# Weight sums of a seven-product step moved from VectorE into adding transfers, with two column sums and one weight split reordered

## The chip, the cores and the metric

The kernel runs on one core of a Trainium2 chip. The metric is the device time of one execution in microseconds (us). A difference of 0.2% is 2.2 us.

## The reference

One layer of an encoder on 256 tokens of width 2048, in float32: a mixer with two groups of eight heads (forgetting attention, "FoX", and stick-breaking attention, "SB"), and a convolutional feed-forward part.

```python
def reference(x, attn_norm, w_in, ..., w_out, ffn_norm, w_up, conv_w, conv_b, w_down):
    for layer in range(DEPTH):                                   # DEPTH = 1
        h = rms_norm(x, attn_norm[layer])
        x = x + hybrid_mixer(h, w_in[layer], ..., w_out[layer])
        h = rms_norm(x, ffn_norm[layer])
        x = x + conv_ffn(h, w_up[layer], conv_w[layer], conv_b[layer], w_down[layer])
    return x

def hybrid_mixer(...):
    ...
    merged = jnp.concatenate([rms_norm(from_heads(out_a), out_norm_fox_l),
                              rms_norm(from_heads(out_b), out_norm_sb_l)], axis=-1)
    return merged @ w_out_l          # (256 x 2048) @ (2048 x 2048)

def conv_ffn(h, w_up_l, conv_w_l, conv_b_l, w_down_l):
    u = h @ w_up_l
    ...                              # causal convolution of width 3
    gate, val = jnp.split(u, 2, axis=-1)
    return (jax.nn.silu(gate) * val) @ w_down_l
```

The change lies in `merged @ w_out_l`, in the rows of w_out that belong to the second group of heads (SB), and in the start of `conv_ffn` right behind it.

## The kernel before, in words

**Matmuls in three passes.** Each operand is split into a high part in a reduced format (`w_hi`, `hT[..., 0, :]`) and a low part, the rest (`w_lo`). A product is high x high, low x high and high x low. For weights the high part is a cast on ScalarE (ACT, L263) and the low part a subtraction on VectorE (DVE, L271), of 128 x 2048 elements each. `in_three` (L291) issues the matmuls on TensorE (PE, and PEld for its weight loads).

**Steps.** The program is a list of steps, one for each piece of weights of 1 MB. A step has a load (on SyncE's queue, SP), perhaps a sum, a split, its matmuls and a "follow", which adds the result to the residual stream `xb` (called `x2` in the code). The loop at the end of the kernel emits for step n: follows that are due, the split of step n + 2 (`SPLIT`), follows again, the load of step n + 6 (`LOAD`), the sum of step n + 4 (`SUM`), then the matmuls of step n, then the transposes that are due (`after`) and a part of the heads (`tick`). Each engine works through its own list in that order.

**w_out in two groups.** Group 0 is FoX, group 1 is SB. Each group's 1024 rows of w_out are multiplied with 2048 columns, in two halves of columns. Columns 0 and 1 (of 512 each, called c=0 and c=1 here) are done plainly in group 1, with the tile `acc_o`, in two steps each (`out_rows`, kh = 0 and 1). Columns 2 and 3 are done by `out_unit` in Strassen's manner: seven products instead of eight, on sums of weight blocks (w11, w12, w21, w22, 1 MB each) and sums of head outputs (`T5`, `S2`, `S4`, `T7`, kept in `oFox` and split into `hT`). In group 1 the steps come in this order, and I call the seven products P1 to P7:

| step of group 1 | work | weights before |
|---|---|---|
| 0 | P1 (bank "a") | w11 |
| 1, 2, 3 | c=0 first half, c=1 first half, c=0 second half (in which the heads end) | plain |
| 4 | P2 (bank "b"), T5 | w11 += w12, by an adding transfer |
| 5 | P3 (bank "bc") | w21 |
| 6 | P4 (bank "a"), S2 | w11 += w22, on DVE (L924) |
| 7 | c=1 second half | plain |
| 8 | P5 (bank "a"), T7 | w12 += w22, by an adding transfer |
| 9 | P6 (bank "b"), S4 | w22 |
| 10 | P7 (bank "a") | w11 += w21, by an adding transfer |

An adding transfer is a DMA on POOL's software queue (`q0` in the profile; L890 for weights, L956 for `xb`) that adds what it brings to what lies there. SP's loads are on a hardware queue (`q1`).

**The norm of the heads.** After c=0's second half, `norm_of_heads` takes the sum of squares on PE (`pg`, L968), works out the factor `rg` on DVE and ACT (`rs_a` L168 to `rg` L176) and its negative `nrg` (L974). Every addition to `xb` needs it. For P1, c=0, P2 and P3 the addition is staged: ACT writes the scaled bank into a `stage` tile (L955) and an adding transfer brings it to `xb`. For c=1 and for P4 to P7, DVE does it (L1035 and L913).

**Into the feed-forward.** When a column of `xb` is finished, `columns_done` has PE transpose it (L192; I write T c0 to T c3; they come in the order c0, c1, c3, c2), ACT squares it (L210), and ACT and DVE make the parts of `hT` (L200, L203). The transposes stand on PE in this place: c=1 second half, T c0, P5, P6, T c1, P7, T c3, then the first piece of w_up (FFN+0, L1252), T c2, and the next pieces.

Of the kernel before, what the change touches and what calls it, by code (L numbers as in the profile page):

```python
# [15 lines left out]
P = 128  # L16
# [29 lines left out]
def hybrid_layer(  # L46
# [219 lines left out]
    def split(raw, a, b):  # L266
        return subtracted(raw, *cast(raw, a * b, act.copy), a, b)
# [36 lines left out]

    def pieces(w, k0, n, c0, cols, matmuls, follow=None, hold=None):

        mem = {}

        def loads():
            mem["raw"] = load(rows_of(w, k0, n, c0, cols))  # L310

        def prepare():
            if hold is None:
                mem["parts"] = split(mem["raw"], n, cols)
            else:
# [554 lines left out]
    def out_unit(group, c0, raw_tokens):  # L870
# [9 lines left out]

        def product(name, new, lhs, weights, to, load_=(), sums=None, plus=None, negative=False, first=False, then=None,
                    finished=None, later=None, staged=False):
            parts = []
            n, t = to

            def loads():
                for key, src in load_:
                    mem[key] = load(src)
                if plus is not None:
                    nc.gpsimd.dma_start(  # L890
                        mem[weights].rearrange("p (a b) -> p a b", a=4), plus, accum_op=ALU.add
                    )

            def prepare():
                parts.extend(split(mem[weights], 4, 512))

# [21 lines left out]

            if later is not None:
                later.append(prepare)  # L920
            new_step(loads, sums, prepare if later is None else None, matmuls, follow)

        def sum_of(other):
            return lambda: dve.tensor_tensor(mem["11"], mem["11"], mem[other], op=ALU.add) and None  # L924

        later = later_splits
        if group == 0:
# [4 lines left out]
            yield product("b", False, fox_sum(S4), "22", (1, 0))  # L932
            yield product("a", False, fox_sum(T7), "12", (1, 1), plus=w22, negative=True)
            yield product("a", False, raw_tokens(1, 1), "11", (0, 1), plus=w21)
# [12 lines left out]
    later_splits, stages = [], []  # L947

    def add_by_transfer(xs, bank, r):
        if not stages:  # L950
            for t in (at.tile([P, WF], F32, name=f"stage{i}", tag=f"v{i}") for i in range(2)):
                stages.extend((t[:, :512], t[:, 512:]))
            stages.append(heads_tile("stage").rearrange("p a b -> p (a b)")[:, :512])
        stage = stages.pop()
        act.activation(stage, bank, AF.Identity, scale=r)  # L955
        nc.gpsimd.dma_start(xs, stage, accum_op=ALU.add)  # L956
# [42 lines left out]
    def out_rows(group, c, kh):  # L999
# [24 lines left out]
        def follow():  # L1024
# [51 lines left out]

    def sums_of_first_heads():
# [4 lines left out]
        yield  # L1082
# [436 lines left out]
```

## Time and profile before

| | us |
|---|---|
| three runs | 1101.57, 1102.04, 1102.05 (median 1102.04) |
| profiled execution | 1101.38 |
| its span on the core | 1099.6 |
| PE busy | 1088.7 (99%) |
| DVE busy | 938.1 (85%) |
| ACT busy | 766.1 (70%) |
| POOL busy | 67.4 (6%) |

Times in the profile are in us from the span's start. An idle time in brackets at a row's end is what the engine waited just before it, with what released it. The stage of the change is from about 330 to 405 us; the feed-forward follows and runs to the end.

### The profile page before, as it was taken

The page shows a single profiled execution, that of the slowest core. Times are in us where ns is not written, and L with a number is a line of the kernel's source. Part 1 is how long each engine was busy: PE and PEld are TensorE (multiplying, and loading weights), DVE is VectorE, ACT ScalarE, POOL GpSimd, SP SyncE. Part 2 cuts the span into 40 slices and gives each one's busy share as a digit, 9 for nine tenths or more (in the row PEclk, how much of TensorE's full clock was granted, in tenths as well). Part 3 has the DMA queues.
Part 4 walks back from the last instruction along what each step waited for, and adds up shares of the span by engine and source line. Part 5 has one row for each costly group of instructions (what it writes and reads, how often), then busy time and mean ns, then how long its engine had stood idle before and what let it go on. Part 6 is the DMA issues. An engine that isn't in the chain of part 4 may idle for free.

```text
span 1099.6 us, 14723 instructions
## 1 busy us (share of the span) xinstructions
PE 1088.7 (99%) x5689; PEld 937.4 (85%) x5689; DVE 938.1 (85%) x933; ACT 766.1 (70%) x984; POOL 67.4 (6%) x61
## 2 busy tenths in 40 slices
PE   9999999999999989999999999999999999999998
PEld 9988888888888778888888888888888888888887
DVE  5988899888899876779888998889898898879996
ACT  6767696767766866767766766776676667666762
POOL 0000000001000200000000010000000000000000
PEclk9999999999999999999999999999999999999999
DMA  8897886868778895569979598996979699895995
GB/s 308 282 273 227 267 217 189 245 192 271 237 218 222 199 286 187 166 192 224 309 203 310 173 276 258 249 287 175 299 203 274 235 240 296 199 317 167 287 262 146
DMA packets 177519, 262.98 MB, mean 239 GB/s; under 512 B 4760, under 2 KB 98346, under 8 KB 177450
## 3 DMA queue, kind: packets, MB, share of 16 engines
q1 hardware_dynamic: 151690, 210.26, 56.3%
q0 software_dynamic: 25584, 51.65, 26.7%
q8 instruction: 45, 0.74, 0.3%
q14 instruction: 24, 0.20, 0.0%
q10 hardware_dynamic: 176, 0.14, 0.0%
HBM read 258.62 MB, written 2.10 MB: 237 GB/s over the span
## 4 chain that ended last, share of the span: by engine, by line
PE 95%; DVE 2%; ACT 1%; issue 1%; DVEq 0%
PE pu L1252 44%; PE bank_a L291 19%; PE bank_b L291 11%; PE bank_c L291 6%; PE acc_v L411 4%; PE acc_o L291 3%; PE bank_e L291 2%; PE acc L291 2%; DVE w_lo L271 1%; ACT w_hi L263 1%; PE ps_h L637 1%; PE ps_o L709 1%; DVE hT L203 0%; PE ps_x L192 0%; PE ps_z L785 0%
## 5 line engine op out<-in xcount | busy, mean ns | idle before, releaser
L271 DVE TENSOR_TENSOR w_lo<-w_raw,w_hi 128x2048 fp32r<-128x2048 f32 (+2 forms) x254 | 562.5, 2219 | 119.4 <-ACT w_hi L263 115.9
L263 ACT CAST w_hi<-w_raw 128x2048 fp32r<-128x2048 f32 (+2 forms) x254 | 470.1, 1854 | 219.6 <-PE pu L1252 94.4
L1252 PE MATMUL pu<-hT,w_hi 128*128 128x512 f32 x1408 | 335.8, 391 | 2.1 <-DVE hT L203 2.0
L1252 PEld LDWEIGHTS pu<-hT,w_hi 128*128 128x128 f32 x1408 | 263.3, 188 | 57.1 <-DVE hT L203 3.0
L1252 PEld LDWEIGHTS pu<-hT,w_lo 128*128 128x128 f32 x1408 | 180.5, 192 | 6.7
L1252 PE MATMUL pu<-hT,w_lo 128*128 128x256 f32 x1408 | 182.4, 283 | 0.0
L1305 POOL DMA_DIRECT2D w_raw<-in_w_down_dram x31 | 39.9, 1305 | 664.8 <-DVE w_lo L271 318.7
L1176 ACT ACTIVATE tap<-up,ccol 128x256 f32<-128x256 f32 x176 | 74.7, 495 | 0.0
L291 PE MATMUL bank_a<-w_hi,hT 128*128 128x512 f32 x208 | 52.7, 395 | 1.3 <-ACT w_hi L263 1.3
L291 PEld LDWEIGHTS bank_a<-w_hi,hT 128*128 128x128 f32 x208 | 38.0, 188 | 9.0 <-ACT w_hi L263 1.7
L291 PE MATMUL bank_b<-w_hi,s 128*128 128x512 f32 x160 | 40.0, 392 | 0.0
L291 PE MATMUL bank_a<-w_hi,s 128*128 128x512 f32 x160 | 40.0, 392 | 0.0
L291 PE MATMUL bank_a<-w_hi,g 128*128 128x512 f32 x152 | 38.0, 392 | 0.0
L411 PE MATMUL acc_v<-w_hi,hT 128*128 128x344 f32 x192 | 35.5, 326 | 0.0
L291 PEld LDWEIGHTS bank_b<-w_hi,s 128*128 128x128 f32 x160 | 28.9, 189 | 5.2
L291 PEld LDWEIGHTS bank_a<-w_hi,s 128*128 128x128 f32 x160 | 28.9, 189 | 5.3
L1181 DVE TENSOR_TENSOR gate<-gate,tap 128x512 f32<-128x512 f32 x44 | 30.3, 688 | 2.3
L1181 DVE TENSOR_TENSOR val<-val,tap 128x512 f32<-128x512 f32 x44 | 30.3, 688 | 2.3
L1162 DVE TENSOR_TENSOR up<-t,R 128x512 f32<-128x512 f32 x44 | 30.5, 692 | 1.5
L291 PEld LDWEIGHTS bank_a<-w_hi,g 128*128 128x128 f32 x152 | 27.4, 189 | 5.0
L1169 ACT ACTIVATE gate<-up,ccol 128x256 f32<-128x256 f32 x44 | 24.1, 594 | 10.1 <-DVE s L1223 5.2
L411 PEld LDWEIGHTS acc_v<-w_hi,hT 128*128 128x128 f32 x192 | 30.3, 188 | 0.6 <-DVE hT L203 0.2
(314 smaller groups left out, 1432.9 us busy)
## 6 DMA issues: line engine op xcount, KB each, us to landing
w_raw<-in_w_up_dram SPq DMA_DIRECT2D x88, 1024.0 KB, 8.2
w_raw<-in_w_down_dram SPq DMA_DIRECT2D x44, 1024.0 KB, 7.0
w_raw<-in_w_in_dram SPq DMA_DIRECT2D x40, 1024.0 KB, 5.6
w_raw<-in_w_down_dram POOLq DMA_DIRECT2D x31, 1024.0 KB, 9.7
w_raw<-in_w_out_dram SPq DMA_DIRECT2D x16, 1024.0 KB, 7.6
w_raw<-in_w_in_dram POOLq DMA_DIRECT2D x10, 1024.0 KB, 9.5
w_raw<-in_w_in_dram SPq DMA_DIRECT2D x13, 516.0 KB, 5.2
w_raw<-in_w_out_dram POOLq DMA_DIRECT2D x5, 1024.0 KB, 9.2
```

Of the source, the lines that this page charges most:

```text
L263: copy(hi[:, :n], raw[:, :n])
L271: dve.tensor_tensor(lo[:, :n], raw[:, :n], f32(hi[:, :n]), op=ALU.subtract)
L291: nc.tensor.matmul(o, lhs(i, l, t), r[:, i, :] if cut is None else r[:, i, cut], start=starts and j == 0, stop=stops and j == 3 * n - 1, s ...
L411: nc.tensor.matmul(banks[j][t][:, :VC], of_half(hT[:, k], l, t), w[:, 0, m * VC : (m + 1) * VC], start=k == l == 0 and w is mem["parts", i ...
L637: nc.tensor.transpose(ps[:, h, :], rows[n, t][:, h * HD : (h + 1) * HD], ident)
L709: mm(po, v, w[:, i, :S], start=m == 0, stop=False)
L1162: dve.tensor_tensor(u[:, :, 2:], t2, R, op=ALU.mult)
L1169: act.activation(a[:, j, :], u[:, j, 2:], AF.Identity, scale=ccol[:, 2, f : f + 1], bias=ccol[:, 3, f : f + 1],)
L1176: act.activation(taps[w][:, j, :], u[:, j, w : w + S], AF.Copy, scale=ccol[:, w, f : f + 1])
L1181: dve.tensor_tensor(a, a, tap, op=ALU.add)
L1252: nc.tensor.matmul(acc[:, j, S:] if low else acc[:, j, :], (lo if low else hi)[:, i, j * P : (j + 1) * P], hT[:, k, 0, :] if low else hT[: ...
L1305: nc.gpsimd.dma_start(mem[weights].rearrange("p (a b) -> p a b", a=4), plus, accum_op=ALU.add)
```

## The change

**Weight sums.** P2's weights get a tile of their own ("5"): w11 is loaded a second time and w12 is added to it by a transfer. P4's weights become w11 + w12 + w22, by two adding transfers on the tile "11" (so the head sums and the bank signs stay as they are), and the sum on DVE goes. POOL's additions of weights in group 1 go from three to five, SP's loads of w_out from 16 to 17. P7's w21 comes later on the same tile, as before.

On POOL, at the place of the second heads, these rows stood before (`w_raw_2851` is the tile "11", `w_raw_3134` the tile "12", the last 2851 the addition of w21; `xb<-stage` is a staged sum):

```order
L890 DMA w_raw_2403<-in_w_out_dram 128x4x512
L890 DMA w_raw_2851<-in_w_out_dram 128x4x512
L890 DMA w_raw_3134<-in_w_out_dram 128x4x512
L956 DMA xb_2502<-stage_3244 128x512
L956 DMA xb_2502<-stage1_3243 128x512 x2
L890 DMA w_raw_2851<-in_w_out_dram 128x4x512
L956 DMA xb_2502<-stage0_3242 128x512 x2
```

And these stand there now (`w_raw_2968` is the new tile "5"):

```order
L892 DMA w_raw_2403<-in_w_out_dram 128x4x512
L892 DMA w_raw_2851<-in_w_out_dram 128x4x512
L892 DMA w_raw_2968<-in_w_out_dram 128x4x512
L892 DMA w_raw_2851<-in_w_out_dram 128x4x512
L892 DMA w_raw_3136<-in_w_out_dram 128x4x512
L965 DMA xb_2502<-stage0_3244 128x512 x2
L965 DMA xb_2502<-stage1_3245 128x512
L892 DMA w_raw_2851<-in_w_out_dram 128x4x512
L965 DMA xb_2502<-stage1_3245 128x512
L965 DMA xb_2502<-stage2_3246 128x512 x2
L965 DMA xb_2502<-stage0_3244 128x512
```

**Additions of c=1.** They are staged too, like those of c=0 (`if group:` instead of `if group > c:`), in six `stage` tiles that go round. On ACT, from the squares of c=0 to the squares of c=3, the order moves like this (the plain `w_hi<-w_raw` rows are casts of weights):

```order
 L210 ACTIVATE spare,ss_122<-xb 128x512 x2
+L964 ACTIVATE stage_3246<-acc_o,rg_126 128x512
+L964 ACTIVATE stage_3244<-acc_o,rg_126 128x512
 L200 ACTIVATE hT<-ps_x,pcol 128x256 x4
-L263 CAST w_hi<-w_raw 128x2048 x2
+L263 CAST w_hi<-w_raw 128x2048
 L210 ACTIVATE spare,ss_122<-xb 128x512 x2
+L263 CAST w_hi<-w_raw 128x2048
 L200 ACTIVATE hT<-ps_x,pcol 128x256 x2
 L263 CAST w_hi<-w_raw 128x2048
```

The two stagings of c=1 now stand ahead of c=0's `hT`; the cast of FFN+0's weights, which stood ahead of the squares of c=1, stands behind them. These squares and T c1 on PE now wait for the two adding transfers of c=1.

**Norm ahead of low weights, and other turns.** P3's cast comes early, and its low part is taken only behind the norm (`late_low`). The head sums of P4 run as its sum (`first_heads_sums`). Follows of group 1's products and of c=1 are put first in their turn (`first`). P7's split is taken at P5's follow and FFN+0's at P6's, out of one list (`later_splits`). On DVE, from the last head sums to P4's low weights, before:

```order
L1087 TENSOR_TENSOR oFox_114<-oFox_114 128x4x128
L1089 SCALAR_TENSOR_TENSOR oFox_114<-oFox_114 128x4x128
L1073 TENSOR_TENSOR hT_94<-oFox_114,hT_94 128x4x128
L271 TENSOR_TENSOR w_lo_3228<-w_raw_3020,w_hi_3227 128x2048
L168 TENSOR_SCALAR rs_a_3231<-pg_3220 128x2
L173 TENSOR_TENSOR rs_u_3233<-rs_a_3231,rs_y_3232 128x2
L174 TENSOR_TENSOR rs_u_3233<-rs_u_3233,rs_y_3232 128x2
L175 TENSOR_SCALAR rs_u_3233<-rs_u_3233 128x2
L176 TENSOR_TENSOR rg1_126<-rs_y_3232,rs_u_3233 128x2
L974 TENSOR_SCALAR nrg1_128<-rg1_126 128x2
```

And the same place now (`w_raw_3022` is P3's tile, `pg` the norm's sums):

```order
L1095 TENSOR_TENSOR oFox_114<-oFox_114 128x4x128
L1082 TENSOR_TENSOR hT_94<-oFox_114,hT_94 128x4x128
L1098 SCALAR_TENSOR_TENSOR oFox_114<-oFox_114 128x4x128
L168 TENSOR_SCALAR rs_a_3233<-pg_3226 128x2
L173 TENSOR_TENSOR rs_u_3235<-rs_a_3233,rs_y_3234 128x2
L174 TENSOR_TENSOR rs_u_3235<-rs_u_3235,rs_y_3234 128x2
L175 TENSOR_SCALAR rs_u_3235<-rs_u_3235 128x2
L176 TENSOR_TENSOR rg1_126<-rs_y_3234,rs_u_3235 128x2
L983 TENSOR_SCALAR nrg1_128<-rg1_126 128x2
L271 TENSOR_TENSOR w_lo_3186<-w_raw_3022,w_hi_3185 128x2048
```

P3's low weights (`w_lo` from tile 3020, now 3022) went from the place ahead of the norm to the place behind it. PE's instructions and their order are the same in both kernels; only what they wait for differs.

The diff, cut to what changes behaviour:

```diff
-    def pieces(w, k0, n, c0, cols, matmuls, follow=None, hold=None):
+    def pieces(w, k0, n, c0, cols, matmuls, follow=None, hold=None, first=False):
...
-        new_step(loads, None, prepare, lambda: matmuls(mem["parts"]), follow)
+        new_step(loads, None, prepare, lambda: matmuls(mem["parts"]), follow, first)
...
             def loads():
                 for key, src in load_:
                     mem[key] = load(src)
-                if plus is not None:
+                for src in plus:
                     nc.gpsimd.dma_start(
-                        mem[weights].rearrange("p (a b) -> p a b", a=4), plus, accum_op=ALU.add
+                        mem[weights].rearrange("p (a b) -> p a b", a=4), src, accum_op=ALU.add
                     )
             def prepare():
-                parts.extend(split(mem[weights], 4, 512))
+                if late_low:
+                    hi, lo = cast(mem[weights], 2048, act.copy)
+                    later.append(lambda: parts.extend(subtracted(mem[weights], hi, lo, 4, 512)))
+                else:
+                    parts.extend(split(mem[weights], 4, 512))
...
-            if later is not None:
+            if late:
                 later.append(prepare)
-            new_step(loads, sums, prepare if later is None else None, matmuls, follow)
+            new_step(loads, sums, None if late else prepare, matmuls, follow, first=group == 1)
...
+        def next_later():
+            later.pop(0)()
...
         yield product("a", True, raw_tokens(0, 0), "11", (0, 0), [("11", w11)], staged=True)
-        yield product("b", True, fox_sum(T5), "11", (1, 1), plus=w12, staged=True)
-        yield product("bc", True, raw_tokens(1, 0), "21", (0, 0), [("21", w21)], staged=True, later=later)
-        yield product("a", False, fox_sum(S2), "11", (1, 0), [("22", w22)], sum_of("22"), negative=True)
+        yield product("b", True, fox_sum(T5), "5", (1, 1), [("5", w11)], plus=[w12], staged=True)
+        yield product("bc", True, raw_tokens(1, 0), "21", (0, 0), [("21", w21)], staged=True, late_low=True)
+        yield product("a", False, fox_sum(S2), "11", (1, 0), sums=first_heads_sums, plus=[w12, w22], negative=True)
         yield product(
-            "a", False, fox_sum(T7), "12", (1, 1), [("12", w12)], plus=w22, negative=True,
-            then=lambda: later.pop()(),
+            "a", False, fox_sum(T7), "12", (1, 1), [("12", w12)], plus=[w22], negative=True, then=next_later,
         )
-        yield product("b", False, fox_sum(S4), "22", (1, 0), finished=3)
-        yield product("a", False, raw_tokens(1, 1), "11", (0, 1), plus=w21, finished=2, later=later)
+        yield product("b", False, fox_sum(S4), "22", (1, 0), [("22", w22)], then=next_later, finished=3)
+        yield product("a", False, raw_tokens(1, 1), "11", (0, 1), plus=[w21], finished=2, late=True)
...
         if not stages:
-            for t in (at.tile([P, WF], F32, name=f"stage{i}", tag=f"v{i}") for i in range(2)):
-                stages.extend((t[:, :512], t[:, 512:]))
-            stages.append(heads_tile("stage").rearrange("p a b -> p (a b)")[:, :512])
-        stage = stages.pop()
+            tiles = [at.tile([P, WF], F32, name=f"stage{i}", tag=f"v{i}") for i in range(2)]
+            tiles.append(heads_tile("stage2").rearrange("p a b -> p (a b)"))
+            stages.extend(t[:, c : c + 512] for t in tiles for c in (0, 512))
+        stage = stages.pop(0)
+        stages.append(stage)
...
-                if group > c:
+                if group:
                     add_by_transfer(xs, acc[t], rgs[group][:, t : t + 1])
...
-            held if (group, c, kh) == (0, 3, 0) else None,
+            held if (group, c, kh) == (0, 3, 0) else None, first=group == c == 1,
...
         high_sum(first_heads, last_tokens)
+        low_sum(first_heads, last_tokens)
         dve.scalar_tensor_tensor(a22, a11, -1.0, a22, op0=ALU.mult, op1=ALU.subtract)
-        low_sum(first_heads, last_tokens)
-        later_splits.pop(0)()
         yield
+        later_splits.pop()()
...
-    hooks[SB_OUT + 2] = lambda: following.append(sums_of_first_heads())
+    later_splits.append(steps[FFN][2])
+    steps[FFN] = steps[FFN][:2] + (None,) + steps[FFN][3:]
```

More of the change, by code (lines that the diff above doesn't have):

```diff
@@ L879, in open_bank, with product @@
             return psb.tile([P, 512], F32, name=f"bank_{name}", tag="t")
-        def product(name, new, lhs, weights, to, load_=(), sums=None, plus=None, negative=False, first=False, then=None,
-                    finished=None, later=None, staged=False):
+        def product(
+            name, new, lhs, weights, to, load_=(), sums=None, plus=(), negative=False, first=False, then=None,
+            finished=None, late_low=False, late=False, staged=False,
+        ):
             parts = []
@@ L932, in out_unit @@
             yield product("b", False, fox_sum(S4), "22", (1, 0))
-            yield product("a", False, fox_sum(T7), "12", (1, 1), plus=w22, negative=True)
-            yield product("a", False, raw_tokens(1, 1), "11", (0, 1), plus=w21)
+            yield product("a", False, fox_sum(T7), "12", (1, 1), plus=[w22], negative=True)
+            yield product("a", False, raw_tokens(1, 1), "11", (0, 1), plus=[w21])
             return
         yield product("a", True, raw_tokens(0, 0), "11", (0, 0), [("11", w11)], staged=True)
-        yield product("b", True, fox_sum(T5), "11", (1, 1), plus=w12, staged=True)
-        yield product("bc", True, raw_tokens(1, 0), "21", (0, 0), [("21", w21)], staged=True, later=later)
-        yield product("a", False, fox_sum(S2), "11", (1, 0), [("22", w22)], sum_of("22"), negative=True)
+        yield product("b", True, fox_sum(T5), "5", (1, 1), [("5", w11)], plus=[w12], staged=True)
+        yield product("bc", True, raw_tokens(1, 0), "21", (0, 0), [("21", w21)], staged=True, late_low=True)
+        yield product("a", False, fox_sum(S2), "11", (1, 0), sums=first_heads_sums, plus=[w12, w22], negative=True)
         yield product(
-            "a", False, fox_sum(T7), "12", (1, 1), [("12", w12)], plus=w22, negative=True,
-            then=lambda: later.pop()(),
-        )
-        yield product("b", False, fox_sum(S4), "22", (1, 0), finished=3)
-        yield product("a", False, raw_tokens(1, 1), "11", (0, 1), plus=w21, finished=2, later=later)
+            "a", False, fox_sum(T7), "12", (1, 1), [("12", w12)], plus=[w22], negative=True, then=next_later,
+        )
+        yield product("b", False, fox_sum(S4), "22", (1, 0), [("22", w22)], then=next_later, finished=3)
+        yield product("a", False, raw_tokens(1, 1), "11", (0, 1), plus=[w21], finished=2, late=True)
     later_splits, stages = [], []
@@ L1075, in low_sum, with first_heads_sums @@
         )
-    def sums_of_first_heads():
+    def first_heads_sums():
         a11, a21 = oFox[:, first_heads, first_tokens], oFox[:, first_heads, last_tokens]
@@ L1081, in sums_of_first_heads @@
         dve.tensor_tensor(a11, a11, a21, op=ALU.subtract)
-        yield
     def sums_of_heads():
```

## The prediction

> **What bounds the kernel now.** I read the page's busy times first, then the chain that ended last, then the stretches of the stage that the change touches, and only then single rows and transfers.
>
> ```profile
> PE 1088.7 (99%) x5689; PEld 937.4 (85%) x5689; DVE 938.1 (85%) x933; ACT 766.1 (70%) x984; POOL 67.4 (6%) x61
> ...
> PE 95%; DVE 2%; ACT 1%; issue 1%; DVEq 0%
> ```
>
> TensorE (PE) works 99% of the span and carries 95% of the chain, and the change leaves PE's own instructions and their order alone. So time can be won only where PE idles, and lost only where a new wait stops it. In the next table, of stretches in the w_out products of the second heads, the columns are the stretch, its length, then busy time of PE, PEld, DVE, ACT and POOL, the granted clock, the DMA share and GB/s.
>
> ```profile
> 352.00:361.70 9.70, 9.70 (x47) 8.09 (x46) 6.43 (x12) 3.95 (x7) 0.03 (x1) 1.00 0.68 113
> 361.70:369.35 7.65, 5.12 (x20) 3.25 (x19) 4.37 (x6) 7.62 (x10) 3.57 (x5) 1.00 0.78 196
> 369.35:381.00 11.65, 11.65 (x55) 9.77 (x56) 11.65 (x13) 9.75 (x13) 2.19 (x3) 1.00 1.05 195
> 381.00:388.00 7.00, 5.28 (x32) 4.29 (x31) 7.00 (x6) 6.75 (x13) 0.00 (x0) 1.00 1.09 357
> 388.00:400.00 12.00, 10.07 (x58) 8.08 (x56) 10.87 (x23) 8.57 (x18) 0.00 (x0) 1.00 1.08 336
> 400.00:405.00 5.00, 4.85 (x23) 4.11 (x24) 0.63 (x3) 1.86 (x2) 0.00 (x0) 0.66 1.02 328
> 405.00:500.00 95.00, 95.00 (x548) 84.03 (x547) 68.08 (x65) 63.67 (x85) 2.62 (x2) 1.00 0.59 180
> ```
>
> PE is never idle up to 361.7 and from 405 on. It idles 7.65 - 5.12 = 2.53 us in the second row, 1.72 in the fourth and 1.93 in the fifth; the sixth runs at a clock of 0.66. These 6.2 us and that clock are all there is to win. The first piece, and what ends it (rows of the timeline: start, length, engine, line; in brackets the idle time and its releaser):
>
> ```profile
> 357.41 0.50 PE L968 MATMUL pg<-cs,ssq 128*128 128x1 f32 x4
> 358.08 2.29 DVE L271 TENSOR_TENSOR w_lo<-w_raw,w_hi 128x2048 fp32r<-128x2048 f32 x1 [1.12 <-ACT w_hi L263]
> 360.29 0.15 DVE L168 TENSOR_SCALAR rs_a<-pg 128x2 f32<-128x2 f32 x1
> 361.73 0.69 ACT L955 ACTIVATE stage<-bank_a,rg 128x512 f32<-128x512 f32 x1 [0.82 <-DVE rg L176]
> 364.79 2.11 PE L291 MATMUL bank_a<-w_hi,hT 128*128 128x512 f32 x8 [1.27 <-ACT w_hi L263]
> 367.11 1.20 PE L291 MATMUL bank_a<-w_lo,hT 128*128 128x512 f32 x4 [0.22 <-DVE w_lo L271]
> 369.35 3.92 PE L291 MATMUL acc_o<-w_hi,oSb 128*128 128x512 f32 x16 [1.04 <-ACT w_hi L263]
> ```
>
> The norm's sums of squares are finished on PE at 357.41 + 0.50 = 357.9, but DVE is in P3's low weights until 360.37, so `rs_a` starts at 360.29 and the staging of P1 at 361.73. P4 then starts 1.27 us late, its low pass 0.22 late and the c=1 rows 1.04 late.
>
> **The change part by part.**
>
> Norm ahead of P3's low weights: that 2.29 us instruction leaves the place ahead of `rs_a`, which can start at 358.0 instead of 360.29, and the norm and the staging behind it come 2.3 us earlier. Low bound of the gain: 0, if the cast of P4 waits for something else (its sum now comes from two adding transfers). High bound: all 2.53. P3's low weights move behind the norm: done at about 359.4 + 2.3 = 361.7, and P3's low pass reads them at 362.44, so that costs nothing, with 0.7 us of cover; gone, it would be the low pass that is late. The c=1 cast still stands behind three stagings on ACT, so I take P4's 1.27 and the 0.22, together 1.5, and keep the 1.04 for the bound.
>
> ```profile
> 343.30 1.91 ACT L263 CAST w_hi<-w_raw 128x2048 fp32r<-128x2048 f32 x1
> 347.56 2.29 DVE L924 TENSOR_TENSOR w_raw<-w_raw 128x2048 f32<-128x2048 f32 x1
> 348.14 0.47 ACT L828 ACTIVATE oSb<-ps_o,pcol 128x256 fp32r<-128x256 f32 x1 [2.94 <-PE ps_o L710]
> ```
>
> The weight sum on DVE (2.29 us at 347.56) goes. PE lost nothing to it, since PE is fully busy there, so it is worth 0. The price of its replacement: P2's cast, at 343.30 before, now reads a tile that is loaded (w11 again) and then added to. ACT waits 2.94 us ahead of `oSb` of a head at 348.14, so the cast of 1.91 may start as late as 346.2 at no cost; later than that, the last head's outputs, and with them the norm, are late by as much. When does that addition land? Software transfers of before:
>
> ```profile
> q0 software_dynamic: 528, 1.05, 86.4%
> w_raw<-in_w_out_dram POOLq DMA_DIRECT2D x1, 1024.0 KB, 8.4
> q1 hardware_dynamic: 1489, 2.96, 99.5%
> q0 software_dynamic: 528, 1.05, 53.0%
> q0 software_dynamic: 466, 0.86, 43.8%
> q1 hardware_dynamic: 1040, 1.05, 27.3%
> q0 software_dynamic: 773, 1.49, 93.3%
> q1 hardware_dynamic: 395, 0.40, 15.6%
> ```
>
> These are the software (q0) and hardware (q1) queues in 333 to 340, in 340 to 348, in 348 to 360, in 360 to 372 and in 372 to 381, with the packets, the MB and the share of the 16 DMA engines; the second row is the addition issued at 331.86, which lands 8.4 us later, at 340.3. In 372 to 381 the two shares add to 1.09, so 1.1 is what a full stretch reads. One addition of 1.05 MB takes 0.530 x 12 / 1.1 to 0.864 x 7 / 1.1 = 5.5 to 5.8 of engine time, and 1.49 MB in 0.933 x 9 / 1.1 = 7.6 is 5.1 per MB; I use 5.2 us per MB. The new addition follows that of 340.3: alone it lands at 340.3 + 5.5 = 345.8; taking turns with the loads, which fill 340 to 348 (99.5%), at up to 347.9. The middle, 346.8, holds the cast 0.6 us. Bounds 0 and 1.7. So the work ahead of T c1 (PE's transposes of the c=1 columns) comes 1.5 - 0.6 = 0.9 us earlier, between -1.7 and 2.53.
>
> P4's two additions land 5.5 and 11 us later, at 351 to 353 and 357 to 359. P4's cast ended just ahead of 364.79 and so began at 362.9, 2.3 earlier now: 360.6. So nothing waits for these two, nor for P5's behind them, but they fill the queue for all that follows.
>
> The additions of c=1 are what I think decides. Before, DVE did them; now ACT stages the two halves and two adding transfers bring them to `xb`:
>
> ```profile
> 378.00 1.40 DVE L1035 SCALAR_TENSOR_TENSOR xb<-acc_o,rg,xb 128x512 f32<-128x512 f32 x2
> 365.67 1.26 ACT L955 ACTIVATE stage<-acc_o,rg 128x512 f32<-128x512 f32 x2
> 375.56 1.57 ACT L200 ACTIVATE hT<-ps_x,pcol 128x256 fp32r<-128x256 f32 x4 [0.70 <-PE ps_x L192]
> 381.26 1.03 PE L192 MATMUL ps_x<-cs,xb 128*128 128x128 f32 x8
> 381.93 0.62 ACT L210 ACTIVATE spare<-xb 128x512 f32<-128x512 f32 x1
> ```
>
> DVE loses 1.40 us at 378; ACT gains 1.26 (the price of the two c=0 stagings), of which 0.70 fills the idle time ahead of `hT` at 375.56, and the rest delays a high part that is not read before the feed-forward. Both are worth 0 by themselves. But PE's T c1 at 381.26 and ACT's squares at 381.93 read these columns and must now wait for the landings. The two transfers stand last on the software queue: behind P1's and c=0's stagings, w21's addition, and P2's and P3's stagings.
>
> ```profile
> 368.34 1.41 POOL L890 DMA_DIRECT2D w_raw<-in_w_out_dram  x1
> 369.09 2.45 POOL L956 DMA_DIRECT2D xb<-stage  x2
> xb<-stage POOLq DMA_DIRECT2D x2, 256.0 KB, 11.5
> xb<-stage POOLq DMA_DIRECT2D x1, 256.0 KB, 12.0
> w_raw<-in_w_up_dram SPq DMA_DIRECT2D x3, 1024.0 KB, 12.9
> w_raw<-in_w_up_dram SPq DMA_DIRECT2D x88, 1024.0 KB, 8.2
> ```
>
> Before, w21's addition is issued at 368.34 and two stagings right behind it; these take 11.5 in the median, and the last, issued at 370.18 within the second row, takes 12.0 and lands at 382.2, although each moves only 256 KB: they stand in line behind w21's 1 MB. The three w_up loads that run then take 12.9 us, against 8.2 over the kernel (the last row, from the page).
>
> What the change adds to this line, in engine time: two more additions (three to five, in the second heads), 2 x 1.05 MB x 5.2 = 10.9; two more stagings, 2 x 0.262 x 5.2 = 2.7; one more load, 1.05 MB at 2.97 MB per 8 us = 2.8. Sum 16.4 us. What the engines have free between 333 and 382.2: 7 x (1 - 0.933 / 1.1) = 1.1 (q0 and q1 together, q1 being 6.9%); 0 in 340 to 348; 12 x (1 - 0.54 / 1.1) = 6.1; 12 x (1 - 0.711 / 1.1) = 4.2; 0 behind 372. Sum 11.4. So 5.0 us don't fit, and the last landing goes from 382.2 to 387.2. Low end: the w_up loads of 360 to 381 (1.45 MB, 27.3% of 12 and 15.6% of 9, over 1.1: 4.3 us) give way wholly: 382.9. High end: of the free time in 360 to 372, a part is gone because the line is issued in lumps; with none of it used, 391.4. I take 386.8, a little under the sum, since the whole line from P1's staging on is issued up to 2 us earlier by the early norm. T c1 then starts at 386.8 instead of 381.26: 5.5 us late. The 0.9 won above lies in front of this wait and is swallowed by it.
>
> Behind T c1 the path to the steady feed-forward is as long as before. These rows and the last of the chain show it:
>
> ```profile
> 386.78 1.06 PE L192 MATMUL ps_x<-cs,xb 128*128 128x128 f32 x8 [1.72 <-issue]
> 400.15 2.95 PE L1252 MATMUL pu<-hT,w_hi 128*128 128x512 f32 x6 [2.00 <-DVE hT L203]
> ```
>
> From T c1 to T c3 (columns c=3) it was 386.78 - 381.26 = 5.52 us, of which T c3 waits 1.72, so 3.8 is work of T c1 and P7. Now the cast of the first w_up weights stands behind the squares of c=1 on ACT: 386.8 + 1.5 of squares (two of 0.62 and their read-outs) + 1.91 of cast + 2.29 of low part on DVE = 392.5. DVE's low part of `hT` for c=1 follows, some 0.4 for one (ACT's 1.57 for four), and frees the PSUM tile that T c3 needs, at 392.7 to 392.9. P7 is done at 386.8 + 3.8 = 390.6. So T c3 waits about 2.2 us, 0.5 more than the 1.72; the bound below is no wait at all, -1.72. The 2.00 ahead of 400.15 (DVE's `hT`) and the slow clock behind it stay: no row says otherwise. I take this part as 0, between its bounds.
>
> Sum: the profiled execution is 1101.38 us (span 1099.6), 0.66 under the median of the runs, 1102.04. 1101.38 + 5.5 = 1106.9, and at the median 1107.5.
>
> **The rivals.** The other side: the landing comes before PE. It decides at T c1's arrival, 381.26 - 0.9 = 380.4. For it: the queue before is idle in parts of 340 to 372, and the norm is early. Against it: 16.4 us of added work would have to fit into 11.4 and the last landing still come 1.8 earlier than before. Then 0.9 is won, and at best T c3's 1.72 too, since DVE has 2.29 + 1.40 us less to do: 1102.04 less 0.9 to 2.6, say 1099.5.
>
> No net change: the landing is at 380.4 to 383.3, around the low end above, so -0.9 to +2.0: 1102.5. For it speaks the 12.9 us of the w_up loads, which pay when both queues run; against it, that the staged transfers take 12.0 too.
>
> The early addition: P2's cast is held the full 1.7 or longer, the last head and the norm come late, and all transfers of staged sums with them, instead of 2.3 early. The line then starts up to 2 us later: 1109.5.
>
> The clock: in 400 to 405 PE's granted clock was 0.66, behind a gap of 2.00 us, while it stayed 1.00 after the 1.72 at 386.78. With a wait of 386.8 - 380.4 = 6.4 us at T c1, the stretch behind it can be slow too. If it lasts like that one (5 us at 0.66), 5 x 0.34 = 1.7 is lost, most of it behind the 2.0 that T c3 waits; without this cover, 1109.2. The Trainium skill, "TensorE: Matmul & The Clock Gate", Part 1, says that PE falls to half its clock after an idle window of about 3.4 us; by that rule the slow stretch comes here and costs half of 3.4, 1.7 as well, an estimate from that page. The trace slows after less idle time than the page asks for.
>
> **How the numbers follow.** Forecast 0.52; late addition or slow clock 0.15; no net change 0.18 (of it a third slower by over 0.2%); other side 0.15. 0.2% is 2.2 us, about what a measurement can tell from no change. Slower: 0.52 + 0.15 + 0.05 = 0.72 less 0.04 for the forecast's own low end, 0.68; same 0.17; faster 0.15. The forecast's own range follows the landing, 383.9 to 390: 1104.7 to 1110.8. The range for all reaches down to the no-change case, 1101.3, which leaves out most of the other side, and up to 1111.3.
>
> **What would show it.** Right: T c1 waits 4 to 8 us with the staged transfer as releaser; the last landing is at 385 to 390; ACT stands in the squares of c=1 until then; P4 starts without the 1.27. Wrong: the last landing is before 382, or T c1 starts without idle time; or the w_up loads grow to 17 us and more while the staged transfers keep their 12; or P2's cast starts before 344, so that the early addition was free; or the steady feed-forward starts by less than the landing is late, because the wait of T c3 has shrunk.

## Result, and the profile after

| | median us | runs | ratio to before, 95% interval |
|---|---|---|---|
| before | 1101.97 | 4 | 1 |
| changed | 1110.07 | 4 | 1.0079 (1.0062 to 1.0097) |

The change made the kernel 8.1 us slower. The profiled execution of the changed kernel took 1112.61 us (span 1110.8), 2.5 above its median, so its waits are a little larger than those of the other runs; the profiled one of before was 0.6 below its own.

The page of the changed kernel, busy times and the chain:

```profile
PE 1091.6 (98%) x5689; PEld 939.6 (85%) x5689; DVE 934.6 (84%) x930; ACT 767.4 (69%) x986; POOL 71.6 (6%) x65
...
PE 95%; issue 2%; DMA 1%; DVE 1%; ACT 1%; POOL 1%; DVEq 0%; POOLq 0%; ACTq 0%
```

A transfer, `DMA xb<-stage`, is now a part of the chain that ended last. The same stretches as before (stretch, length, busy time of PE, PEld, DVE, ACT, POOL, granted clock, DMA share, GB/s):

```profile
352.00:361.70 9.70, 7.27 (x35) 5.81 (x34) 7.88 (x15) 5.10 (x11) 0.21 (x1) 1.00 1.02 335
361.70:369.35 7.65, 7.61 (x33) 5.74 (x31) 7.03 (x10) 6.27 (x9) 3.18 (x5) 1.00 0.83 147
369.35:381.00 11.65, 9.60 (x45) 7.65 (x45) 8.86 (x8) 9.67 (x14) 5.36 (x6) 1.00 1.11 246
381.00:388.00 7.00, 2.90 (x13) 2.06 (x11) 2.15 (x4) 1.90 (x1) 0.00 (x0) 1.00 1.11 234
388.00:400.00 12.00, 8.14 (x34) 6.32 (x34) 7.78 (x7) 8.80 (x18) 0.00 (x0) 0.72 1.09 341
400.00:405.00 5.00, 4.84 (x29) 4.18 (x30) 5.00 (x11) 3.63 (x7) 0.00 (x0) 1.00 0.39 127
```

PE idles 2.43 us in the first row, where it was never idle before, next to nothing in the second (2.53 before), 2.05 in the third (0 before), 4.10 in the fourth (1.72) and 3.86 in the fifth (1.93), and the fifth has a clock of 0.72. Of the 2.53 us that could be won, a part was won and more was lost elsewhere. The timeline of the changed kernel shows where:

```profile
336.57 17.93 SPq L257 DMA_DIRECT2D w_raw<-in_w_out_dram  x4
349.87 1.91 ACT L263 CAST w_hi<-w_raw 128x2048 fp32r<-128x2048 f32 x1 [6.23 <-DMA w_raw<-in_w_out_dram]
355.02 0.70 PE L821 MATMUL ps_o<-w,vB 128*128 128x256 f32 x2 [2.43 <-ACT w L809]
360.89 0.16 DVE L168 TENSOR_SCALAR rs_a<-pg 128x2 f32<-128x2 f32 x1 [0.37 <-PE pg L977]
361.49 1.28 POOL L892 DMA_DIRECT2D w_raw<-in_w_out_dram  x1 [19.11 <-DVE rs_a L168]
366.30 1.97 PE L291 MATMUL bank_a<-w_hi,hT 128*128 128x512 f32 x8
370.82 3.92 PE L291 MATMUL acc_o<-w_hi,oSb 128*128 128x512 f32 x16 [1.29 <-ACT w_hi L263]
377.43 0.98 PE L192 MATMUL ps_x<-cs,xb 128*128 128x128 f32 x7 [0.76 <-DMA xb<-stage]
384.99 1.90 ACT L263 CAST w_hi<-w_raw 128x2048 fp32r<-128x2048 f32 x1 [4.19 <-DMA w_raw<-in_w_out_dram]
386.61 0.75 DVE L919 SCALAR_TENSOR_TENSOR xb<-bank_a,nrg,xb 128x512 f32<-128x512 f32 x1 [4.85 <-DMA xb<-stage]
390.10 0.63 ACT L210 ACTIVATE spare<-xb 128x512 f32<-128x512 f32 x1 [3.21 <-DMA xb<-stage]
390.26 0.45 PE L192 MATMUL ps_x<-cs,xb 128*128 128x128 f32 x1 [6.36 <-DVE xb L919]
391.85 1.76 PE L192 MATMUL ps_x<-cs,xb 128*128 128x128 f32 x7 [1.14 <-DMA xb<-stage]
393.26 2.91 PE L291 MATMUL bank_a<-w_hi,oSb 128*128 128x512 f32 x8
```

Read in order: P2's cast waits 6.23 us for its addition and starts at 349.87 instead of 343.30. The heads' work behind it on ACT is late, PE waits 2.43 us at 355.02, and the norm's `rs_a` starts at 360.89, 0.6 later than before and not 2.3 earlier. P4 (366.30) has lost its 1.27 us wait, the c=1 rows (370.82) wait 1.29 (1.04 before). T c0 waits for a staged transfer. P7's cast (384.99) waits 4.19 us for the addition of w21, and P5's addition on DVE (386.61) 4.85 for P2's staged transfer, which adds to the same columns. The squares of c=1 (390.10) and T c1 wait for c=1's two transfers, landing at 390.0 and 391.8; the profile puts the first wait of T c1 (390.26) to DVE, which ended then too. The last landing is in the chain:

```profile
379.63 12.17 DMA xb<-stage
```

P7 starts at 393.26, and before it started here:

```profile
382.05 2.10 PE L291 MATMUL bank_a<-w_hi,oSb 128*128 128x512 f32 x8
```

It is 11.2 us late, and that is the whole difference of the two spans.

Why P2's addition came so late, from the transfers of the changed kernel (packets, MB, share of the engines for 341.5 to 349.5; then the addition issued at 335.5 and the load issued at 336.6 with their time to landing; then 381 to 390):

```profile
q0 software_dynamic: 525, 1.04, 70.6%
q1 hardware_dynamic: 494, 1.00, 37.9%
w_raw<-in_w_out_dram POOLq DMA_DIRECT2D x1, 1024.0 KB, 14.3
w_raw<-in_w_out_dram SPq DMA_DIRECT2D x1, 1024.0 KB, 14.5
q0 software_dynamic: 678, 1.23, 73.9%
q1 hardware_dynamic: 940, 0.95, 35.8%
```

The addition is issued at 335.5, stands behind the one before until 340.6, and then runs packet by packet with the loads, 525 against 494; it lands after 14.3 us, at 349.8, at 130 KB/us. The loads pay too: the one issued at 336.6 takes 14.5 us, where that of before took 6.7. The load of w12 is the third in the row at 336.57, issued at 343.5 as before; but P5's addition, which needs it landed, is issued at 361.49 instead of 350.75. The profile names `rs_a` as what released that addition; but the trace also has a mark for each of the 16 DMA engines when its part of a transfer is in, and the last mark of w12's load stands at 360.94, and at 350.19 before, 0.6 us ahead of the issue in both. All staged sums stand behind that addition on the queue. From 381 to 390 the packets are 678 to 940 only because the last staged transfer runs out: in the last of these 9 us they are 35 to 283, and 643 to 657 in the eight ahead of it.

### The profile page after: what moved, and what is told of

Same layout as the page of the kernel before. It is cut to its first block, busy times and chain, and to the rows that moved or that the text cites. A ratio compares the mean times of both kernels' runs of the same rounds, so it can differ in the third digit from the quotient of the medians.

```text
span 1110.8 us, 14739 instructions
## 1 busy us (share of the span) xinstructions
PE 1091.6 (98%) x5689; PEld 939.6 (85%) x5689; DVE 934.6 (84%) x930; ACT 767.4 (69%) x986; POOL 71.6 (6%) x65
## 4 chain that ended last, share of the span: by engine, by line
PE 95%; issue 2%; DMA 1%; DVE 1%; ACT 1%; POOL 1%; DVEq 0%; POOLq 0%; ACTq 0%
PE pu L1260 43%; PE bank_a L291 18%; PE bank_b L291 10%; PE bank_c L291 6%; PE acc_v L411 4%; PE acc_o L291 3%; PE bank_e L291 2%; PE acc L291 2%; DMA xb<-stage 1%; PE ps_h L637 1%; PE ps_o L709 1%; ACT w_hi L263 0%; POOL xb L965 0%; PE ps_x L192 0%; DVE w_lo L271 0%
```

## Experiments

Times are medians, ratios are against runs of the kernel before on the same chip.

### c=1 back on DVE (e1)

```diff
-                if group:
+                if group > c:
                     add_by_transfer(xs, acc[t], rgs[group][:, t : t + 1])
```

> The changed kernel with one part undone: the additions of c=1 are DVE's again, the five adding transfers of weights stay. Theory of the line (the software queue is too long, whatever stands in it): the wait at T c1 goes, but P7's cast still waits for the addition of w21, which landed at 385.0 in the changed kernel, so P7 starts at about 387 instead of 393.3, and 382.05 before. Time 1104 to 1107 us. Rival, the new wait for c=1's transfers alone: P7 is on time too, and the time is that of before, 1101 to 1102.5. Rival, the early addition alone (P2's cast held, TensorE idle for 2.43 us at 355): the idle time at 355 stays in both cases; if it were all, the time would stay above 1108.

Measured: 1107.29 us, ratio 1.0047 (1.0033 to 1.0062). Its timeline:

```profile
349.01 1.91 ACT L263 CAST w_hi<-w_raw 128x2048 fp32r<-128x2048 f32 x1 [5.18 <-DMA w_raw<-in_w_out_dram]
354.16 0.70 PE L821 MATMUL ps_o<-w,vB 128*128 128x256 f32 x2 [1.39 <-ACT w L809]
377.18 0.98 PE L192 MATMUL ps_x<-cs,xb 128*128 128x128 f32 x7 [1.54 <-DMA xb<-stage]
384.81 1.90 ACT L263 CAST w_hi<-w_raw 128x2048 fp32r<-128x2048 f32 x1 [5.42 <-DMA w_raw<-in_w_out_dram]
386.52 0.75 DVE L919 SCALAR_TENSOR_TENSOR xb<-bank_a,nrg,xb 128x512 f32<-128x512 f32 x1 [5.89 <-DMA xb<-stage]
387.42 2.08 PE L291 MATMUL bank_a<-w_hi,oSb 128*128 128x512 f32 x8 [2.88 <-ACT spare L210]
```

P7 starts at 387.42, as the line theory had it (387), though T c1 waits for no transfer any more. w21's addition lands just as late, so the cast ends at 386.7; and P5's addition on DVE, which frees P7's bank, waits 5.89 us for P2's staged transfer behind w21 and ends at 387.3. (The squares that the profile names at 387.42 ended then too.) Without the staged additions of c=1 the change still costs 0.5%. PE also waits 1.39 us at 354.16, for the early addition, and 1.54 at T c0; what these two cost by themselves isn't shown, since P7 waits for the line behind them.

### Weight sums back on DVE (e2)

```diff
-        yield product("b", True, fox_sum(T5), "5", (1, 1), [("5", w11)], plus=[w12], staged=True)
+        yield product("b", True, fox_sum(T5), "11", (1, 1), plus=[w12], staged=True)
...
-        yield product("a", False, fox_sum(S2), "11", (1, 0), sums=first_heads_sums, plus=[w12, w22], negative=True)
+        yield product("a", False, fox_sum(S2), "11", (1, 0), [("22", w22)], lambda: (sum_of("22")(), first_heads_sums())[0], negative=True)
...
-        yield product("b", False, fox_sum(S4), "22", (1, 0), [("22", w22)], then=next_later, finished=3)
+        yield product("b", False, fox_sum(S4), "22", (1, 0), then=next_later, finished=3)
```

> The changed kernel with the other part undone: P2's weights are added in place on w11 and P4's sum is DVE's, as before; so three weight additions and 16 loads. The additions of c=1 stay staged. Theory of the line: without 2 MB of additions and 1 MB of load the last landing comes at 382.2 + 2 x 0.262 x 5.2 = 385, less up to 1.5 for an earlier norm: T c1 at 383.5 to 385, 2 to 4 us late, 1103 to 1106 us. Rival, the wait for c=1's transfers alone: T c1 is as late as in the changed kernel, 1109 to 1110. Rival, the early addition: it is gone, so 1100 to 1102.

Measured: 1105.98 us, ratio 1.0039 (1.0026 to 1.0052). T c1 in its timeline:

```profile
384.56 0.45 PE L192 MATMUL ps_x<-cs,xb 128*128 128x128 f32 x1 [3.90 <-DMA xb<-stage]
386.26 1.75 PE L192 MATMUL ps_x<-cs,xb 128*128 128x128 f32 x7 [1.25 <-DMA xb<-stage]
```

The time is at the upper end of the line theory. The last landing, 386.26, is 1.3 later than its upper number, so the staged transfers take longer than 1.36 us each; e4 and e7 bear on that.

### Both back on DVE (e3)

The two edits above together.

> Both parts undone; what is left of the change is the norm ahead of P3's low weights, the turns of the follows and the late splits of P7 and of the first w_up piece. Theory of the line: no new wait is left, rs_a starts at about 358.0 instead of 360.3, P4's 1.27 us of idle time goes, 1099.5 to 1101. Rival: the reordering is worth nothing or costs at T c3, 1101.5 to 1103.

Measured: 1100.41 us, ratio 0.9980 (0.9969 to 0.9990). Three rows of its timeline:

```profile
358.43 0.16 DVE L168 TENSOR_SCALAR rs_a<-pg 128x2 f32<-128x2 f32 x1 [0.37 <-PE pg L977]
363.84 1.98 PE L291 MATMUL bank_a<-w_hi,hT 128*128 128x512 f32 x8
368.20 3.92 PE L291 MATMUL acc_o<-w_hi,oSb 128*128 128x512 f32 x16 [1.29 <-ACT w_hi L263]
```

The norm starts at 358.43, P4 without a wait, and the c=1 rows keep their 1.29. This is faster than both kernels: what is left of the change, the norm ahead of P3's low weights and the turns, is its only good part. It also gives the prices against the same base, by medians: from 1100.41, the weight sums by transfer add 6.9 us (e1), the staged c=1 5.6 (e2), and both 9.7 (the changed kernel), less than the sum of 12.5, since the waits that they make, at P7 and at T c1, lie side by side.

### c=1 staged in the kernel before (e4)

```diff
-                if group > c:
+                if group:
                     add_by_transfer(xs, acc[t], rgs[group][:, t : t + 1])
```

with the six rotating stage tiles of the change.

> The kernel before with one part done alone: the additions of c=1 are staged and brought by adding transfers, in six stage tiles; nothing else. Theory of the line: the last landing goes from 382.2 to 382.2 + 2.7 = 384.9 or a little later, T c1 starts there instead of at 381.26, and the time is 1104.5 to 1107 us. Rival, hidden: 1101.5 to 1102.5. Rival, the wait for c=1's transfers alone explains the whole loss: 1109 to 1110.

Measured: 1108.98 us, ratio 1.0058 (1.0043 to 1.0074); its profiled execution took 1109.62. T c1, and the two queues from 377 to 379:

```profile
386.92 0.45 PE L192 MATMUL ps_x<-cs,xb 128*128 128x128 f32 x1 [5.49 <-DMA xb<-stage]
388.61 1.75 PE L192 MATMUL ps_x<-cs,xb 128*128 128x128 f32 x7 [1.25 <-DMA xb<-stage]
q0 software_dynamic: 165, 0.30, 80.5%
q1 hardware_dynamic: 166, 0.17, 30.2%
```

All my numbers were too small here: 388.61 against 384.9 expected. The queue is the same, but two more transfers cost 6.4 us, not 2.7. Software and hardware packets go 165 to 166 while both run; so each further staged transfer also lets through w_up packets. That explains about half: by the trace's marks the second of the two lands 1.8 us behind the first (388.57 against 386.78), so two at that pace are 3.6. The first lands 4.7 us behind P3's transfer (382.09), because the software queue pauses. Both were issued by 377.83, but it sends 7 packets in 381 to 383, against 744 hardware ones, and none from 381.70 to 383.11. What holds it there isn't shown.

### The same with the w_up loads left out (e7)

Five pieces of w_up (the second to the sixth) aren't loaded and use the first piece's weights, so the computation is another one; only the landings are read.

```diff
-                mem["raw"] = load(rows_of(wu, 8 * kh, 8, c0, 2 * P))
+                if 0 < step < 6:
+                    mem["raw"] = first_raw[0]
+                else:
+                    mem["raw"] = load(rows_of(wu, 8 * kh, 8, c0, 2 * P))
+                first_raw.append(mem["raw"])
```

> The kernel before with c=1 staged (which measured 1109, last landing at 388.6), and with the loads of five pieces of w_up left out, the second to the sixth: they use the first piece's weights. So the software queue runs alone from 372 to 390. Theory of turn-taking (a software packet for each hardware packet): four staged transfers behind w21's landing at 378.1 need 1.3 to 1.4 us each instead of 2 to 2.6, T c1 runs at 383.5 to 384.5. Rival, the line alone (the software queue has this rate whatever runs beside it): T c1 stays at 388 to 389.

One run, 1103.34 us. T c1, and the software queue from 377.5 to 379.5:

```profile
384.06 0.98 PE L192 MATMUL ps_x<-cs,xb 128*128 128x128 f32 x7 [0.89 <-DMA xb<-stage]
q0 software_dynamic: 228, 0.41, 114.1%
```

T c1's last wait ends at 384.06 instead of 388.61, inside the numbers of the theory. Alone, the queue moves 0.41 MB in 2 us, 205 KB/us; beside the loads in e4 it moved 0.30 MB, 150 KB/us. So the 5.2 us per MB that I used is about what holds where no load runs. But the run doesn't show turn-taking by itself: the pause of e4 is gone as well. By these rates four transfers of 0.262 MB take 7.0 us in turns, and here they took 5.5 (378.5 to 384.0); so turns are some 1.5 of the 4.5 us, and the pause most of the rest. This is an estimate, from one execution.

### c=0 behind w21 (e8, e9)

e8 is e3 with c=0's follow three turns later:

```diff
             if group > c:
-                yield
+                for _ in range(3):
+                    yield
...
-                for _ in range((5, 2)[c]):
+                for _ in range((3, 2)[c]):
```

> The version with both parts undone (1100.4), with c=0's two stagings moved behind the cast of the c=1 rows on ACT. By that their adding transfers are issued behind w21's addition instead of ahead of it; no byte is added. Theory of the line (order on the queue decides): c=0's columns land behind w21, at 378 to 381, T c0 waits for them from 373.8 on, 1104 to 1107 us, although TensorE's 1.29 us ahead of the c=1 rows go. Rival, the queue's order is free and only the traffic counts: those 1.29 us are won, 1099 to 1100.

Measured: 1105.15 us, ratio 1.0031 (1.0021 to 1.0040).

```profile
366.18 1.46 POOL L892 DMA_DIRECT2D w_raw<-in_w_out_dram  x1
367.82 2.66 POOL L965 DMA_DIRECT2D xb<-stage  x3 [0.18 <-issue]
378.80 1.75 PE L192 MATMUL ps_x<-cs,xb 128*128 128x128 f32 x7 [1.27 <-DMA xb<-stage]
```

In e3 the same places read:

```profile
365.50 1.76 POOL L965 DMA_DIRECT2D xb<-stage  x2 [3.76 <-ACT stage L964]
373.78 1.04 PE L192 MATMUL ps_x<-cs,xb 128*128 128x128 f32 x8
```

The two transfers of c=0 (the first two of the three at 367.82) are issued 2.3 and 2.1 us later than in e3, but behind the 1 MB of w21, and T c0 waits until 378.80 (373.78 in e3). P2's staged transfer goes ahead of w21 in their place. Not a byte was added, and the median is 4.7 us above that of e3. The later issue alone can't be it: in e3 the second one landed 4.2 us behind its issue (366.29 to 370.54), and with that from 368.40 on it would land at 372.6, ahead of T c0's 373.78. It landed at 378.76. The 4.2 is carried over from another run, so this is an estimate. The 1.29 ahead of the c=1 rows went, as expected, and were no use.

e9 was to bring w21's addition behind them, by issuing it from a later place in the program (a hook behind the step in which c=0 is staged).

> The version with c=0's stagings behind the cast of the c=1 rows (which measured 1105.2, T c0 waiting until 378.8), with one more move: w21's addition is issued behind c=0's two transfers and not ahead of them. Theory of the line (order on the queue decides): c=0 lands at 372 to 374 again, T c0 waits at most 1 us, the 1.29 us ahead of the c=1 rows are won, w21 lands about 1 us later and P7's cast with it, which eats a part: 1099 to 1100.5 us. Rival, the late staging itself made that version slow, not its place behind w21: it stays at 1104 to 1106.

Measured: 1104.54 us, ratio 1.0027 (1.0018 to 1.0036).

```profile
366.12 1.47 POOL L933 DMA_DIRECT2D w_raw<-in_w_out_dram  x1
367.76 2.66 POOL L971 DMA_DIRECT2D xb<-stage  x3 [0.18 <-issue]
```

The edit did not move it: w21 (366.12) still stands ahead of c=0 (367.76). POOL's list isn't in the program's order, since the kernel gives only PE, DVE, ACT and SP to `manual_schedule`. So e9 is e8 once more and says nothing on the rival; whether c=0 staged late but ahead of w21 would gain stays open.

### Four additions, c=1 on DVE (e5)

```diff
-        yield product("b", True, fox_sum(T5), "5", (1, 1), [("5", w11)], plus=[w12], staged=True)
+        yield product("b", True, fox_sum(T5), "11", (1, 1), plus=[w12], staged=True)
...
-        ... sums=first_heads_sums, plus=[w12, w22], negative=True)
+        ... sums=first_heads_sums, plus=[w22], negative=True)
```

and `group > c` as in e1. The addition of w22 comes onto the tile before P2's cast has read it, so P2's weights hold w22 as well.

> As the version with both parts undone (1100.4), but P4's sum is made by one adding transfer of w22 instead of DVE; P2's weights are added in place, so there is no second load of w11 and no copy: four weight additions. Theory of the early addition: without the copy, P2's cast starts at about 344 and TensorE is not idle at 355; the one added transfer fits into the idle time of the queue between 341 and 362, and w21 lands as before: 1100 to 1101 us. Rival, the line is too long with every additional MB: w21 is 3 to 5 us late, P7 waits, 1103 to 1105.

Measured: 1110.12 us, ratio 1.0080 (1.0067 to 1.0094).

```profile
357.12 1.90 ACT L263 CAST w_hi<-w_raw 128x2048 fp32r<-128x2048 f32 x1 [12.99 <-DMA w_raw<-in_w_out_dram]
362.26 1.22 PE L821 MATMUL ps_o<-w,vB 128*128 128x256 f32 x2 [9.20 <-ACT w L809]
```

Neither expectation fits, since P2's cast now waits for both additions, until 357.12. PE then waits 9.20 us behind it. This shows what a late cast of P2 does: with no new load and c=1 on DVE, it is 13.8 us later than before (343.30), twice as late as in the changed kernel, and PE's wait of 9.20 is about the whole loss, 9.7 us above e3. It does not tell what one more addition costs that nobody waits for; that wasn't measured.

### Only the norm ahead of the low weights (e6)

```diff
...
-        yield product("bc", True, raw_tokens(1, 0), "21", (0, 0), [("21", w21)], staged=True, later=later)
+        yield product("bc", True, raw_tokens(1, 0), "21", (0, 0), [("21", w21)], staged=True, late_low=True)
...
-        later_splits.pop(0)()
         yield
+        later_splits.pop()()
```

in the kernel before, with `late_low` in `product` as in the change.

> The kernel before with one part done alone: P3's cast early and its low part behind the norm; no other turn moved, no transfer added. If the norm's place is what made the version with both parts undone faster: rs_a at about 358.0, P4 without its 1.27 us of idle time, 1100.2 to 1101 us. Rival, the turns of the follows and the late splits made it: 1101.5 to 1102.5.

Measured: 1100.63 us, ratio 0.9991 (0.9981 to 1.0000).

```profile
358.43 0.16 DVE L168 TENSOR_SCALAR rs_a<-pg 128x2 f32<-128x2 f32 x1 [0.98 <-PE pg L972]
```

The norm starts at 358.43 as in e3. The gain is some 0.1%, at the edge of what these intervals can tell. A part of the spread is PE's granted clock: its mean over an execution is 1.00 in some and 0.998 or a little less in others. Compared at the same clock (3 to 16 executions each), e6 is 1.3 us faster than the kernel before at 0.998 (medians 1100.74 and 1102.06) and 0.9 at 1.00 (1099.95 and 1100.81), and e3 1.6 (1100.73 and 1102.28) and 2.0 (1098.78 and 1100.82). So the norm's place is most of the gain; whether the turns add the rest isn't separated.

## Why the prediction was right or wrong

**Direction held, and so did the wait that the forecast named.** Slower, by T c1's wait for the last staged transfer of c=1; ACT stood ahead of the squares of c=1 until 390.10. 1110.07 lies inside 1101.3 to 1111.3, and 2.6 above the 1107.5. Its lying there owes something to luck. The upper end, 1111.3, wasn't worked out from a row, and the execution that was traced, with 1112.61, lies above it. With 8.1 us lost where 5.5 was summed, the size was a third too small.

**What the forecast left out is a second path to P7.** It had P7 follow T c1 at once. But w21's addition also holds P7's cast (384.99 to 386.9), and P2's staged transfer holds P5's addition on DVE, which frees P7's bank, until 387.4. In the changed kernel T c1 hides both; e1 takes T c1's wait away, and P7 still starts 5.4 us late. So the staging of c=1 alone isn't the cause: it adds 2.8 us to what the weight sums cost without it (9.7 against 6.9 above e3).

**The step that failed is the early addition:** "The middle, 346.8, holds the cast 0.6 us. Bounds 0 and 1.7." It landed at 349.8, outside my bounds. I had 5.5 us for it alone and 7.6 at most beside the loads; it took 9.2 behind its predecessor, as its packets went one for one with the loads. I also priced only the additions' side of the turns. The loads lose too, so w12 came late and P5's addition went from 350.75 to 361.49, at the head of the line that I took to start earlier than before. So the rival of the early addition, given less than 0.15, came true together with the forecast and not in its place. "P4's two additions land 5.5 and 11 us later" was miscounted as well: the first of the two is the one that lands at 340.6, ahead of P2's, and only one follows, at 357.8. Nothing waited for it, and the sum of 16.4 doesn't use it.

**The norm's gain** was about right by itself (`rs_a` at 358.43 in e3 and e6, from 360.29, where 358.0 was predicted) and lost in the changed kernel, where `rs_a` starts at 360.89. P4's 1.27 went, as said; the c=1 rows kept theirs, as said.

**The last landing** was put at 386.8 and came at 391.8 (profiled execution). I summed engine time at 5.2 us per MB. With turn-taking the same MB takes about 7 us while loads are there (w21 and the four staged transfers behind it, 2.1 MB, landed one after the other between 377.4 and 391.8), and the line began late, by the step above. The trace before has 245 against 244 packets in 377 to 380; I took nothing from it, and this was the number that sized the term. One of the signs of being wrong came half true: the three w_up loads issued in 372 to 381 took 19.5 us (12.9 before) and gave way, while c=1's two transfers took 11.6; that didn't save T c1.

**Behind T c1** I expected T c3 to wait 2.2 us. It waits about 0.3, but T c1 and P7 ran at a low clock, so the sum of this part was near 0, as said: from P7's 11.2 us the loss goes to 11.0 at the first steady w_up matmul (415.91 against 404.91). The clock of 0.53 in 388 to 391 and 0.50 in 391 to 394 came with an idle time of 6.4 us, which ended at 390.26:

```profile
388.00:391.00 3.00, 0.45 (x1) 0.18 (x1) 2.22 (x2) 0.72 (x2) 0.00 (x0) 0.53 1.09 312
391.00:394.00 3.00, 2.15 (x9) 2.06 (x10) 0.00 (x0) 2.11 (x3) 0.00 (x0) 0.50 1.09 359
```

That is what the Trainium skill, "TensorE: Matmul & The Clock Gate", Part 1, states for an idle window of about 3.4 us, and its half clock is the number seen here. Its price was mostly covered, as the rival said: P7's first row took 2.91 us instead of 2.10, and T c3 lost its wait of 1.72.

The slow stretch behind the 2.00 us at 400.15, which the forecast kept, isn't fixed either: e3 has the same wait (1.98 us at 399.01) with a clock of 1.00 in 396 to 402.

**The rival on the other side** needed a last landing before 380.4; with the weight sums undone it was 386.3 (e2), so it was never near.

The arbitration between queues is told in the Trainium skill, "DMA: Bandwidth & Descriptors", section "Queues, rings and completion order": each engine goes round the queues that have work, a packet from each. The 525 to 494, 165 to 166 and 643 to 657 packets agree with equal turns. The 7 to 744 in 381 to 383 of e4, with two software transfers issued, don't.

## What to carry to other kernels

A sum moved from an engine that nobody waits for into an adding transfer isn't free because the engine gets time back: price it by the place on its queue, and by who waits for the last transfer on that queue. Estimate a transfer's time beside loads by equal turns of packets, and not by the engine time it needs alone. The loads lose by it as well as the additions, so follow them too: what waits for those loads is late as well.

## What the runs showed of the hardware that was not expected

In this stage of every trace here, transfers on the software queue landed in the order of their issue, and a small one waits for a large one ahead of it: moving c=0's two of 256 KB behind w21's 1 MB (e8) shifted T c0, which needs them, by 5.0 us (373.78 to 378.80) with no more traffic, at 2.2 us later issue.

They ran at 205 KB/us alone (0.41 MB in 2 us, e7) and at 130 to 150 KB/us beside loads, and equal turns give both of the lower numbers. In the changed kernel an adding packet held an engine for 0.172 us (70.6% of 16 engines for 8 us, over 525 packets) and the load's packet beside it for 0.098 (37.9%, 494); 0.172 of 0.270 of 205 is 131. In 377 to 379 of e4 it is 0.156 and 0.058, and 149.

Where the loads filled the engines, a transfer issued behind others could also start late: c=1's in e4 (issued from 377.25 on, the next software packet at 383.11), and c=0's in the changed kernel (issued at 368.12, no software packet from 371.63 to 373.28). From 379 to 388 of e4 the software queue so sent 430 packets (0.77 MB) against 1804; why it pauses isn't shown.

An idle time of 2 to 3 us can halve PE's clock for a while or leave it: behind 2.00 us it was 0.50 from 400.3 to 403.7 before, behind 1.98 in e3 it stayed 1.00, and behind 2.88 in e1 as well (387.4 to 392).
